# A hybrid encoder trunk on one NeuronCore: a fourth seven-product group in the feed-forward stages two to four

## The chip, the cores and the metric

The kernel runs on one core of a Trainium2 chip. The metric is the device time of one execution in microseconds, as the median of three runs. One further execution was recorded by the hardware profiler; all rows of the profile come from that one. The engines are named as the profile names them: PE (TensorE matmul), PEld (its weight load), DVE (VectorE), ACT (ScalarE), POOL (GpSimd), SP (SyncE).

## The reference

Two layers; in each a gated feed-forward block, a mixer with two kinds of attention, and a second gated feed-forward block, all on 256 tokens of width 1024 in float32, with a hidden width of 2816. Cut to what this change touches:

```python
def rms_norm(x, g):
    y = xf * lax.rsqrt(jnp.mean(xf * xf, axis=-1, keepdims=True) + RMS_EPS)
    return (y * g).astype(x.dtype)

def swiglu(h, w_gate, w_up, w_down):
    return (jax.nn.silu(h @ w_gate) * (h @ w_up)) @ w_down

for l in range(DEPTH):                                   # DEPTH = 2
    x = x + 0.5 * swiglu(rms_norm(x, ffn1_norm[l]), ffn1_w_gate[l], ffn1_w_up[l], ffn1_w_down[l])
    ...                                                  # the mixer: x = x + concat(oA, oB) @ w_out
    x = x + 0.5 * swiglu(rms_norm(x, ffn2_norm[l]), ffn2_w_gate[l], ffn2_w_up[l], ffn2_w_down[l])
return rms_norm(x, final_norm)
```

So there are four feed-forward stages: the first and second of layer 0, then the first and second of layer 1. In the profile the second lies between about 280 and 460 us, the third between about 460 and 640, the fourth from about 740 to the end.

## The kernel before

**Matmuls in three parts.** Every operand is split into a high part (rounded to fp32r) and a low part (the rest), and a product is taken as high x high + low x high + high x low. ACT makes the high part by a cast, DVE the low part by a subtraction. For a weight block the pair is one "split": `emit_split` (line 175) takes half of a raw block (two of its four 128-row slices, 128 x 1024 elements) and writes the tiles `w` from the tile `raw`. The activations are split in the same way, by `split` (line 507).

**The list of weight blocks.** All weight blocks of 512 KB to 1 MB stand in one list, `specs`, in the order in which PE uses them. `ahead` (line 212) walks through it with three pointers: it issues loads on SP (`emit_dma`, at most six raw tiles at a time), runs a block's preparation (`prep`), and splits halves, up to `look[0]` halves ahead of PE's use. It is called each time a block is taken (`weights`, line 233) and at a block's middle (`Split.part`). What it emits is placed in the queues of ACT, DVE, SP and POOL at that point of the program, and each engine keeps the program's order.

**A feed-forward stage** (`ffn`, line 567) takes the hidden width in five groups of 512 and a rest of 256. In a plain group gate and up take four blocks, each of 24 matmuls (four 128-row slices, two halves of the tokens, three parts). Then h = silu(gate) * up is made (`gate`, `hidden`), transposed on PE and split into the two tiles hT[0] and hT[1] (`turn`), and in the course of the next group two "down" blocks of 24 matmuls add hT's part of the output.

**Groups by seven products.** Groups 2, 3 and 4 compute gate and up in Strassen's way. With a = gate rows 0 to 511, d = gate rows 512 to 1023, b and c the same of up, and the tokens in two halves, seven products of 12 matmuls (`prod`, line 589) take the place of eight. `seven` (line 115) lists the blocks: a, b, d, c and a down block, then three more uses of the tile of a, which by then holds sums, and the second down block. b gets c added by a gather-add, a transfer that adds to what it finds, issued on POOL (`gather`); a gets b added in the same way; c and d are added to a by DVE (`plus`). `by_seven` (line 599) takes the products and combines them on DVE. The activations of the products with sums come from `make_sums` (line 333): four sums of quarters of x, each made on DVE, copied to its high part by ACT and reduced to its low part by DVE. They need a copy of x with its gain in float32, `copies` (line 323), eight instructions on ACT from the transposed x in PSUM. Both are done in the course of group 1, which is plain.

**Statistics of the norm.** `Norm.stats` (line 368) reduces the squares on DVE and takes the power -0.5 on POOL. This comes in the middle of group 0; the gates of group 0 use it as a scale.

**Look-ahead.** In stages two to four it is 8 halves in groups 0 to 2, 7 in group 3 and 6 in group 4; in the first stage 8 in groups 0 and 1, 6 in groups 2 and 3 and 5 in group 4.

## Time and profile before

| | |
|---|---|
| runs | 928.3, 928.95, 928.85 us; median 928.85 |
| the profiled execution | 928.39 us, span 926.6 us, granted TensorE clock 0.999 |
| DMA | 194.58 MB, mean 210 GB/s; loads on SP's queue 53.1% and gather-adds on POOL's 15.4% of the 16 engines' span |
| loads of the feed-forward weights | 1 MB each, a median of 5.3 to 5.6 us from issue to landing |
| gather-adds | 24 of 1 MB, median 10.4 us from issue to landing |

Almost every instruction has line 50, that of the helper `Kept`, through which the program calls the engines; so rows are told apart by their tiles: `ps` is PSUM, `w` a split weight half, `raw` a raw weight block, `s` a tile of activations (split x, h and hT are all of them `s`), `q` and `v` the sums of the activations, `tmp` scratch, `r` the power of the norm. A row of the timeline has start, duration, engine, line, operation, tiles (out<-in), shapes, count, and in brackets the idle time before it and what ended that. A row with a count joins equal instructions that follow each other; its duration runs from the first start to the last end. Ends of matmuls are modelled and overlap, so a rate is read from start to start.

### The profile page before, as it was taken

The numbers are of one execution on the slowest core, as the hardware profiler recorded it, in microseconds if no ns is written. First come the engines' busy times: TensorE is split into PE (matmuls) and PEld (weight loads), VectorE is DVE, ScalarE is ACT, GpSimd is POOL, SyncE is SP. The second block draws the span as 40 slices with busy tenths as digits, with TensorE's granted clock in tenths as the row PEclk, the third lists the DMA queues.
The fourth block names the chain that finished last, engine by engine and source line by source line (L and its number), as shares of the span: only waits on it lengthen the run. The fifth ranks groups of instructions, "written<-read, shape, count | busy, mean of one in ns | idle before, by whom it ended". The sixth has DMA issues, their size and how long they took to land.

```text
span 926.6 us, 12551 instructions
## 1 busy us (share of the span) xinstructions
PE 915.1 (99%) x4732; PEld 771.7 (83%) x4732; DVE 760.8 (82%) x1074; ACT 568.7 (61%) x893; POOL 59.5 (6%) x77
## 2 busy tenths in 40 slices
PE   8999999999999999999999999999999999999997
PEld 6888887899888888888888888888998888888886
DVE  6759999969876579999776799996698676799994
ACT  7836675557755557576475466565578475566561
POOL 0500000000000001000000000000001000001011
PEclk9999999999999999999999999999999999999999
DMA  9986897827434859797767597887462377597731
GB/s 338 358 224 195 253 279 262 239 98 222 135 124 167 255 152 264 188 261 270 260 234 194 144 298 204 252 279 204 114 226 92 137 231 197 143 292 221 229 118 46
DMA packets 110893, 194.58 MB, mean 210 GB/s; under 512 B 3566, under 2 KB 31280, under 8 KB 110832
## 3 DMA queue, kind: packets, MB, share of 16 engines
q1 hardware_dynamic: 96528, 166.74, 53.1%
q0 software_dynamic: 12928, 25.46, 15.4%
q10 hardware_dynamic: 1376, 1.57, 0.5%
q8 instruction: 37, 0.61, 0.3%
q14 instruction: 24, 0.20, 0.1%
HBM read 192.71 MB, written 1.05 MB: 209 GB/s over the span
## 4 chain that ended last, share of the span: by engine, by line
PE 84%; DVE 9%; issue 2%; DMA 2%; ACT 1%; POOLq 0%; ACTq 0%; POOL 0%; DVEq 0%
PE ps L50 84%; DVE w L50 6%; DMA raw<-in_ffn_w_up_dram 2%; DVE tmp L50 2%; DVE raw L50 1%; ACT w L50 1%; DVE s L50 1%; DMA xk<-in_x_dram 0%; ACT s L50 0%; DVE xk L50 0%; POOLq L1077 0%; ACTq L50 0%; ACT tmp L50 0%; POOL rf L50 0%; DVEq L50 0%
## 5 line engine op out<-in xcount | busy, mean ns | idle before, releaser
L50 PE MATMUL ps<-w,s 128*128 128x512 f32 (+1 forms) x2754 | 640.9, 391 | 0.5 <-DVE w L50 0.5
L50 PEld LDWEIGHTS ps<-w,s 128*128 128x128 f32 x2754 | 512.1, 188 | 106.5 <-DVE w L50 1.2
L50 DVE TENSOR_TENSOR w<-raw,w 128x1024 fp32r<-128x1024 f32 (+1 forms) x440 | 461.1, 1095 | 58.8 <-ACT w L50 57.8
L50 ACT CAST w<-raw 128x1024 fp32r<-128x1024 f32 (+1 forms) x440 | 390.8, 948 | 90.6 <-DVE raw L50 68.1
L50 PE MATMUL ps<-w,q 128*128 128x512 f32 x432 | 101.9, 389 | 0.0
L50 PEld LDWEIGHTS ps<-w,q 128*128 128x128 f32 x432 | 81.1, 188 | 16.8
L50 PE MATMUL ps<-s,w 128*128 128x256 f32 x672 | 84.0, 285 | 0.0
L50 PEld LDWEIGHTS ps<-s,w 128*128 128x128 f32 x672 | 81.7, 192 | 1.1
L50 ACT ACTIVATE s<-ps,gcol 128x256 fp32r<-128x256 f32 (+1 forms) x80 | 31.4, 488 | 44.6 <-PE ps L50 42.9
L50 DVE TENSOR_TENSOR raw<-raw,raw 128x1024 f32<-128x1024 f32 x48 | 56.5, 1218 | 0.0
L50 POOL DMA_DIRECT2D raw<-in_ffn_w_up_dram x24 | 31.1, 1295 | 352.5 <-DVE w L50 166.5
L50 ACT CAST s<-ps 128x512 fp32r<-128x512 f32 x44 | 23.9, 592 | 40.7 <-PE ps L50 40.7
L50 DVE TENSOR_TENSOR s<-ps,s 128x512 fp32r<-128x512 f32 x44 | 28.4, 683 | 19.9 <-ACT s L50 19.9
L50 PE MATMUL ps<-ident,s 128*128 128x128 f32 x304 | 40.5, 274 | 0.6 <-DVE s L50 0.6
L50 PEld LDWEIGHTS ps<-ident,s 128*128 128x128 f32 x304 | 35.0, 140 | 6.9 <-DVE s L50 1.5
L50 ACT ACTIVATE tmp<-tmp,r 128x512 f32<-128x512 f32 x24 | 17.3, 722 | 33.8 <-DVE tmp L50 33.8
L50 ACT ACTIVATE s<-s,negm 128x256 f32<-128x256 f32 x64 | 31.9, 501 | 6.6 <-DVE negm L50 6.4
L50 PE MATMUL ps<-w,v 128*128 128x512 f32 x144 | 34.6, 389 | 0.0
L50 ACT CAST q<-tmp 128x512 fp32r<-128x512 f32 x20 | 12.4, 621 | 35.0 <-DVE tmp L50 34.9
L50 PEld LDWEIGHTS ps<-w,v 128*128 128x128 f32 x144 | 27.0, 188 | 5.6
L50 DVE SCALAR_TENSOR_TENSOR s<-ps,gcol,s 128x256 fp32r<-128x256 f32 x48 | 20.3, 478 | 12.1 <-ACT s L50 12.0
L50 ACT COPY tmp<-ps 128x512 f32<-128x512 f32 x28 | 16.3, 583 | 22.5 <-PE ps L50 22.0
(106 smaller groups left out, 419.5 us busy)
## 6 DMA issues: line engine op xcount, KB each, us to landing
raw<-in_ffn_w_down_dram SPq DMA_DIRECT2D x44, 1024.0 KB, 5.5
raw<-in_ffn_w_gate_dram SPq DMA_DIRECT2D x39, 1024.0 KB, 5.6
raw<-in_ffn_w_up_dram SPq DMA_DIRECT2D x39, 1024.0 KB, 5.3
raw<-in_ffn_w_up_dram POOLq DMA_DIRECT2D x24, 1024.0 KB, 10.4
raw<-in_w_in_dram SPq DMA_DIRECT2D x14, 1024.0 KB, 5.4
raw<-in_ffn_w_gate_dram SPq DMA_DIRECT2D x8, 512.0 KB, 6.4
raw<-in_ffn_w_up_dram SPq DMA_DIRECT2D x8, 512.0 KB, 7.4
raw<-in_w_in_dram SPq DMA_DIRECT2D x8, 512.0 KB, 5.3
```

What stands on the lines that cost most here:

```text
L50: ins = issue(*a, **k)
```

## The change

In stages two to four group 1 is computed by seven products as well. The first stage keeps groups 2 to 4. In group 1 the order differs: a and d, the two products with plain operands, come first, then the first down block, then b + c and the others. The float32 copy of x and the first sums are made in group 0, right after the statistics; the low half of a sum comes one step after its high half. Gather-adds are held back from the start of a stage's end (or of the output projection) until the norm's power has been issued on POOL (`issue`, `flush`, `hold`). The look-ahead of groups 1 to 4 in stages two to four is 8, 7, 6 and 5 halves. There are six scratch buffers where there were five, and the squares use one of them in place of a buffer of their own.

```diff
-SEVEN = (2, 3, 4)
+SEVEN = ((2, 3, 4), (1, 2, 3, 4))
...
-        return [Step(4, 512, load(a), key=a, free=[]),
-                Step(4, 512, load(b), key=b, behind=gather(c, b), prep=gather(b, a)),
-                Step(4, 512, load(d), key=d, free=[]),
-                Step(4, 512, load(c), key=c, free=[]),
-                downs[0],
+        bc = Step(4, 512, load(b), key=b, behind=gather(c, b))
+        rest = [Step(4, 512, load(d), key=d, free=[]), Step(4, 512, load(c), key=c, free=[]), downs[0]]
+        steps = [rest[0], rest[2], bc, rest[1]] if first else [bc] + rest
+        steps[0].prep = lambda: issue(gather(b, a))
+        return [Step(4, 512, load(a), key=a, free=[])] + steps + [
                 Step(4, 512, None, src=a, free=[]),
                 Step(4, 512, None, prep=plus(c, a), src=a, free=[c]),
                 Step(4, 512, None, prep=plus(d, a), src=a, free=[a, d]),
                 downs[1]]
...
         if s.behind is not None:
-            s.behind()
+            issue(s.behind)
+    pending, hold = [], [False]
+    def issue(add):
+        pending.append(add)
+        if not hold[0]:
+            flush()
+    def flush():
+        hold[0] = False
+        while pending:
+            pending.pop(0)()
...
                 act.copy(sm[:, :, 0:P], v)
-                dve.tensor_tensor(sm[:, :, P:S], v, f(sm[:, :, 0:P]), op=ALU.subtract)
+            def low(i, v):
+                dve.tensor_tensor(self.sm[i][:, :, P:S], v, f(self.sm[i][:, :, 0:P]), op=ALU.subtract)
             s1 = make(b1, t1, ALU.subtract)
+            s2 = make(s1, t0, ALU.add)
+            low(0, s1)
             yield
-            s2 = make(s1, t0, ALU.add)
+            v = make(t1, t0, ALU.subtract)
+            low(1, s2)
             yield
...
             pool.tensor_tensor(self.r, ms, mhalf[:, 0:2], op=ALU.pow)
+            flush()
...
+            else:
+                w = weights()
+                next(sums, None)
+                p1 = prod(norm.quarter(0, 0), w)
+                hT = turn(h, (0,))
+                w = weights()
+                next(sums, None)
+                act.copy(m1, p1)
+                p2 = prod(norm.quarter(0, 1), w)
+                hT += turn(h, (1,))
+                w = weights()
+                next(sums, None)
+                g0 = put(flat(), p2, m1, ALU.add)
+                silu(g0, g0, 0)
+                down(hT, 0, 0, w)
+                act.copy(m7, prod(norm.summed(2), weights()))
+                p3 = prod(norm.summed(3), weights())
...
-        tokens(gs, norm.xs, weights(), 4)
+        w = weights()
+        sums = iter(())
+        if 1 in sevens:
+            norm.copies()
+            sums = norm.make_sums()
+        tokens(gs, norm.xs, w, 4)
         g = gate(gs)
-        tokens(us, norm.xs, weights(), 4)
+        w = weights()
+        next(sums, None)
+        tokens(us, norm.xs, w, 4)
         h = hidden(g, us)
...
-                look[0] = IN_FFN - max(0, n - 2) if before is not take_x else IN_MIX - (n == NGRP - 1)
-                h = by_seven(h, n)
+                look[0] = IN_FFN + min(sevens) - n if before is not take_x else IN_MIX - (n == NGRP - 1)
+                h = by_seven(h, n, sums)
```

More of the change, by code (lines that the diff above doesn't have):

```diff
@@ L78, in blk, with tmp @@
         return s4.tile([P, 2, 512], dt, tag="s4", name=nm_("s4"))
-    def tmp(tag="tmp", bufs=5, shape=(P, 2, 256), dt=F32):
+    def tmp(tag="tmp", bufs=6, shape=(P, 2, 256), dt=F32):
         return tp.tile(list(shape), dt, tag=tag, bufs=bufs, name=nm_(tag))
@@ L113, in plain, with seven @@
         return Step(kn, n, lambda t: [(t, src)], **how)
-    def seven(wg, wu, c0, downs):
+    def seven(wg, wu, c0, downs, first):
         a, b, c, d = [object() for _ in range(4)]
@@ L243, in trunk, with ffn_specs @@
     for l in range(DEPTH):
-        def ffn_specs(wg, wu, wd):
+        def ffn_specs(wg, wu, wd, sevens):
             down = lambda g, h: plain(wd[l], h * 512, 512, 4 * g, 4)
@@ L249, in ffn_specs @@
                 downs = [down(g - 1, h) for h in range(2)]
-                if g in SEVEN:
-                    specs.extend(seven(wg[l], wu[l], g * 512, downs))
+                if g in sevens:
+                    specs.extend(seven(wg[l], wu[l], g * 512, downs, g == 1))
                 else:
@@ L261, in ffn_specs @@
             specs.append(down(NGRP - 1, 1))
-        ffn_specs(g1, u1, d1)
+        ffn_specs(g1, u1, d1, SEVEN[l > 0])
         wi = w_in[l]
@@ L284, in trunk, with __init__ @@
         fine.update(range(mixed + 2, len(specs)))
-        ffn_specs(g2, u2, d2)
+        ffn_specs(g2, u2, d2, SEVEN[1])
     xk = const.tile([P, 2, D], F32, name="xk")
     class Norm:
-        def __init__(self, g0, sums=len(SEVEN) > 0):
+        def __init__(self, g0, sums=True):
             self.g0, self.xs, self.sums = g0, [], sums
@@ L298, in squares @@
         def squares(self, t, c, n):
-            j_ = tmp("junk", 1, (P, 512))
+            j_ = tmp().rearrange("p a n -> p (a n)")
             act.activation(j_[:, :n], xk[:, t, c:c + n], AF.Square, accum_out=self.ss[:, t, c // 256:c // 256 + 1])
@@ L344, in make @@
                 act.copy(sm[:, :, 0:P], v)
-                dve.tensor_tensor(sm[:, :, P:S], v, f(sm[:, :, 0:P]), op=ALU.subtract)
                 self.sm.append(sm)
                 return v
+            def low(i, v):
+                dve.tensor_tensor(self.sm[i][:, :, P:S], v, f(self.sm[i][:, :, 0:P]), op=ALU.subtract)
             s1 = make(b1, t1, ALU.subtract)
+            s2 = make(s1, t0, ALU.add)
+            low(0, s1)
             yield
-            s2 = make(s1, t0, ALU.add)
+            v = make(t1, t0, ALU.subtract)
+            low(1, s2)
             yield
-            make(t1, t0, ALU.subtract)
+            b0_ = make(b0, s2, ALU.subtract)
+            low(2, v)
             yield
-            make(b0, s2, ALU.subtract)
+            low(3, b0_)
             yield
@@ L565, in late, with ffn @@
                 self.nxt.stats()
-    def ffn(norm, aside=None, before=None, final=False):
+    def ffn(norm, aside=None, before=None, final=False, sevens=SEVEN[1]):
         def silu(out_, acc, t):
@@ L597, in prod, with by_seven @@
             return acc
-        def by_seven(h, g):
+        def by_seven(h, g, sums):
             flat = lambda: tmp().rearrange("p a n -> p (a n)")
@@ L608, in by_seven @@
             m1, m7 = flat(), flat()
-            act.copy(m1, prod(norm.quarter(0, 0), weights()))
-            act.copy(m7, prod(norm.summed(2), weights(held=True)))
-            hT = turn(h, 2)
-            p2 = prod(norm.quarter(0, 1), weights())
-            g0 = put(flat(), p2, m1, ALU.add)
-            p3 = prod(norm.summed(3), weights())
-            silu(g0, g0, 0)
-            down(hT, g - 1, 0, weights())
+            if g > 1:
+                act.copy(m1, prod(norm.quarter(0, 0), weights()))
+                act.copy(m7, prod(norm.summed(2), weights(held=True)))
+                hT = turn(h, 2)
+                p2 = prod(norm.quarter(0, 1), weights())
+                g0 = put(flat(), p2, m1, ALU.add)
+                p3 = prod(norm.summed(3), weights())
+                silu(g0, g0, 0)
+                down(hT, g - 1, 0, weights())
+            else:
[10 more added lines that the diff above has]
+                next(sums, None)
+                g0 = put(flat(), p2, m1, ALU.add)
+                silu(g0, g0, 0)
+                down(hT, 0, 0, w)
+                act.copy(m7, prod(norm.summed(2), weights()))
+                p3 = prod(norm.summed(3), weights())
             h = blk(F32)
             p5 = prod(norm.summed(0), weights())
-            late = g == max(SEVEN)
+            late = g == max(sevens)
             p6 = prod(norm.summed(1), weights(look[0] - 5 if late else 0, late))
@@ L636, in turn @@
             out_ = []
-            for i in range(n):
+            for i in (range(n) if isinstance(n, int) else n):
                 sl = halves(bank())
@@ L664, in ffn @@
         before(2)
-        tokens(gs, norm.xs, weights(), 4)
+        w = weights()
[4 more added lines that the diff above has]
+        tokens(gs, norm.xs, w, 4)
         g = gate(gs)
-        tokens(us, norm.xs, weights(), 4)
+        w = weights()
+        next(sums, None)
+        tokens(us, norm.xs, w, 4)
         h = hidden(g, us)
         for n in range(1, NGRP):
-            sums = norm.make_sums() if n + 1 == min(SEVEN, default=0) else iter(())
-            if n in SEVEN:
-                look[0] = IN_FFN - max(0, n - 2) if before is not take_x else IN_MIX - (n == NGRP - 1)
-                h = by_seven(h, n)
+            if n in sevens:
+                look[0] = IN_FFN + min(sevens) - n if before is not take_x else IN_MIX - (n == NGRP - 1)
+                h = by_seven(h, n, sums)
                 continue
+            sums = norm.make_sums()
             gs = [bank(), bank()]
@@ L713, in ffn_end @@
         look[0] = IN_MIX
+        hold[0] = True
         w = {0: weights()}
@@ L965, in out_part @@
             tokens(accs[h], oT, w, k0, range(2), order=order, h=h)
+        hold[0] = True
         for k0 in (0, 2, 4):
@@ L997, in trunk @@
         final = l == DEPTH - 1
-        parts = ffn(norm, attention_constants, take_x) if l == 0 else ffn(norm)
+        parts = ffn(norm, attention_constants, take_x, sevens=SEVEN[0]) if l == 0 else ffn(norm)
         norm_m = Norm(16 + l * 8, False)
```

## The prediction

> **What bounds the kernel now.** I read the page first, then the busy time by stretch, then each engine in order of time in the second feed-forward stage (280 to 460 us), the first of the three that change.

> ```profile
> span 926.6 us, 12551 instructions
> PE 915.1 (99%) x4732; PEld 771.7 (83%) x4732; DVE 760.8 (82%) x1074; ACT 568.7 (61%) x893; POOL 59.5 (6%) x77
> PE 84%; DVE 9%; issue 2%; DMA 2%; ACT 1%; POOLq 0%; ACTq 0%; POOL 0%; DVEq 0%
> ```

> PE holds 84% of the chain of waits, so a matmul taken away is time won, as long as nothing makes PE wait. DVE's 82% is a mean over unlike stretches (columns: length, then PE, PEld, DVE, ACT and POOL busy with counts):

> ```profile
> 310.00:343.50 33.50, 33.50 (x154) 27.80 (x153) 23.81 (x27) 19.34 (x29) 1.28 (x1) 1.00 0.69 186
> 374.00:405.00 31.00, 31.00 (x142) 25.76 (x141) 30.38 (x32) 19.65 (x23) 2.57 (x2) 1.00 0.80 238
> 405.00:436.00 31.00, 31.00 (x143) 25.75 (x142) 30.86 (x34) 20.11 (x24) 0.00 (x0) 1.00 0.81 246
> ```

> The first row is group 1, plain: DVE has 9.7 us to spare. The others are groups 3 and 4, already by seven products: DVE is full (30.4 and 30.9 of 31), and PE gets through them only because DVE enters with weights split ahead. The change turns the one group with a reserve into such a group.

> **What it takes away.** Group 1 in stages two to four has 84 matmuls for gate and up instead of 96.

> ```profile
> 293.42 22.03 PE L50 MATMUL ps<-w,s 128*128 128x512 f32 x96
> 315.29 1.04 PE L50 MATMUL ps<-ident,s 128*128 128x128 f32 x8
> 355.18 5.60 PE L50 MATMUL ps<-w,s 128*128 128x512 f32 x24
> 360.62 5.60 PE L50 MATMUL ps<-w,q 128*128 128x512 f32 x24
> ```

> 24 matmuls take 360.62 - 355.18 = 5.44, one 0.227; 12 are 2.72, and 36 in three stages **8.2 us**. The eight transposes stay (0.8, from 315.29 to the next matmul at 316.08).

> **What it adds.** Per stage DVE gets six more weight halves to split (18, was 12), four additions of raw weights and seven combinations of products; ACT gets six more casts and two copies; POOL two more gather-adds of 1 MB. The four sums of the activations move from the later part of group 1 to before its products. SP issues as many loads as before, with d and a down block ahead of b. DVE's rows:

> ```profile
> 301.82 2.36 DVE L50 TENSOR_TENSOR w<-raw,w 128x1024 fp32r<-128x1024 f32 x2
> 309.77 1.40 DVE L50 SCALAR_TENSOR_TENSOR s<-ps,hr,tmp 128x512 f32<-128x512 f32 x2
> 316.54 1.29 DVE L50 TENSOR_TENSOR s<-ps,s 128x512 fp32r<-128x512 f32 x2 [3.10 <-ACT s L50]
> 323.17 0.68 DVE L50 TENSOR_TENSOR tmp<-s,s 128x512 f32<-128x512 f32 x1
> 324.55 0.69 DVE L50 TENSOR_TENSOR q<-tmp,q 128x512 fp32r<-128x512 f32 x1 [0.69 <-ACT q L50]
> 352.73 2.35 DVE L50 TENSOR_TENSOR raw<-raw,raw 128x1024 f32<-128x1024 f32 x2
> 360.22 9.16 DVE L50 TENSOR_TENSOR w<-raw,w 128x1024 fp32r<-128x1024 f32 x8
> ```

> A split has its result after 1.2 and holds the queue for 1.14 (9.16 for eight); an addition of raw weights 1.15; a combination 0.6, with its result after 0.7. That is 6 x 1.14 + 4 x 1.15 + 7 x 0.6 = 15.6 us more for DVE, against the reserve of 9.7. The totals alone would cost little, since DVE also idles in group 0; what costs is the order.

> In the program as built, DVE's queue after the statistics of the norm reads: two splits of the first down block, the split of the summed block b + c, sums s1 and s2, low half of s1, second split of b + c, **then** the two products that make h of group 0, two splits of c with two more sum operations between, low half of hT[0], two splits of a + b with a sum operation and a low half, two raw additions, low half of hT[1]. PE wants h after one product, hT[0] after two, hT[1] after 12 matmuls more. Before, PE ran group 0's h through a whole plain group before hT was needed.

> And b + c is a gather-add on POOL, now held back until the norm's power has been issued there, so nothing of it moves before 301.7 (its issue takes 1.3 of POOL, which has nothing else queued but the next gathers):

> ```profile
> 301.01 0.69 POOL L50 TENSOR_TENSOR r<-ms,mhalf 128x2 f32<-128x2 f32 x1 [38.92 <-DVE ms L50]
> 307.24 1.34 POOL L50 DMA_DIRECT2D raw<-in_ffn_w_up_dram  x1 [5.53 <-DMA raw<-in_ffn_w_up_dram]
> ...
> raw<-in_ffn_w_up_dram POOLq DMA_DIRECT2D x1, 1024.0 KB, 9.3
> raw<-in_ffn_w_up_dram POOLq DMA_DIRECT2D x1, 1024.0 KB, 8.0
> raw<-in_ffn_w_up_dram POOLq DMA_DIRECT2D x1, 1024.0 KB, 14.5
> ```

> The landing rows are windows round the gathers at 307, 528 and 42 us: 9.3 with loads beside it, 8.0 the shortest, 14.5 in the first stage with a second gather 6 us behind. Here too a second one (b added to a) stands right behind. I take 9.3, nearest in place and traffic: landed at 311.0. The bounds are 309.7 and 316.2.

> [...]

> ACT's rows for the same place:

> ```profile
> 296.11 4.84 ACT L50 CAST w<-raw 128x1024 fp32r<-128x1024 f32 x5
> 303.96 1.28 ACT L50 ACT_TABLE_LOAD   x1 [3.02 <-PE ps L50]
> 305.26 1.27 ACT L50 ACTIVATE tmp<-ps,r 128x512 f32<-128x512 f32 x2
> 306.42 3.89 ACT L50 CAST w<-raw 128x1024 fp32r<-128x1024 f32 x4
> 316.88 3.04 ACT L50 ACTIVATE s<-ps,gcol 128x256 f32<-128x256 f32 x8
> 323.89 0.62 ACT L50 CAST q<-tmp 128x512 fp32r<-128x512 f32 x1 [0.92 <-DVE tmp L50]
> 346.38 0.59 ACT L50 COPY tmp<-ps 128x512 f32<-128x512 f32 x1 [3.29 <-PE ps L50]
> ```

> The eight copies of the transposed x (3.04) move to just before the gates. There ACT waits 3.02 for PE at 303.96 anyway, so I cost them at nothing; uncovered they would delay the gates by up to 3 us, which h's later wait absorbs. A cast is 1.0, a copy 0.6. From 306.5 ACT stands at the cast of b + c until it lands, and behind it stand ACT's other casts, DVE's split and, in DVE's queue, h.

> **The chain, on the clock of the second stage.** PE ends group 0 24 matmuls before 315.29, at 309.8; the first product ends at 312.5 and PE turns to h.
> - Landed 311.0; cast 1.05, split 1.2, s1 0.7, s2 0.7, copy of s2 0.6, second cast 1.05, second split 1.2, two products 1.4: h at 318.9. **Wait 1: 6.4.**
> - PE: transposes 0.4, product 2.7, transposes 0.4, at hT[0] by 322.4. DVE and ACT from 318.9: split of c 1.1, sum 0.7, its copy 0.6, cast 1.0, split 1.2, low half 0.7: 324.2. **Wait 2: 1.8.**
> - PE: 12 matmuls, 326.9. DVE and ACT from 324.2: split of a + b 1.1, sum 0.7, copy 0.6, copy of the first product 0.5, cast 1.0, split 1.2, two raw additions 2.3, low half 0.7: 332.3. PE does one matmul with the high half in between. **Wait 3: 5.2.**

> Without the ACT hand-overs in it wait 3 is still 1.1 + 0.6 + 0.6 + 1.1 + 2.3 + 0.7 = 6.4 less 2.7 = 3.7, its lower bound. After it DVE has weights ahead again: by the same addition group 2 starts with the lead that group 3 had. So groups 2 to 4 run as 3 and 4 did, with one more to eat from the lead, at 7, 6 and 5 halves of look-ahead instead of 8, 7 and 6. What a lead eaten up costs is shown by the first stage, which runs on 6, 6 and 5:

> ```profile
> 132.63 0.98 PE L50 MATMUL ps<-ident,s 128*128 128x128 f32 x7 [0.34 <-DVE s L50]
> 150.97 9.37 PE L50 MATMUL ps<-w,s 128*128 128x512 f32 x40 [0.54 <-DVE w L50]
> ```

> 0.9 us there; I take 0.5 per stage, bounds 0 and 1.5. Stages three and four have the same queues after the norm's power (rows at 479.33 and 755.95 below), so the stage counts three times. The first stage keeps groups 2 to 4; there only the sums' low halves come one step later, and a sixth scratch buffer replaces one of its own for the squares: DVE's 0.69 wait before a low half (row 324.55) may go, 0 to 0.7 per sum with PE's lead over it; I take 0.

> ```profile
> 479.33 0.71 POOL L50 TENSOR_TENSOR r<-ms,mhalf 128x2 f32<-128x2 f32 x1 [77.99 <-DVE ms L50]
> 755.95 0.70 POOL L50 TENSOR_TENSOR r<-ms,mhalf 128x2 f32<-128x2 f32 x1 [39.00 <-DVE ms L50]
> ```

> **Sum.** Per stage 6.4 + 1.8 + 5.2 + 0.5 - 2.7 = +11.2, three times +33.6. The profiled execution took 928.39 (span 926.6 and 1.8 around it), 0.46 under the median 928.85: 928.4 + 33.6 = **962 us**. Its own range: landing 1.3 earlier or 1.5 later, wait 3 at 3.7, the tail 0 to 1.5: 952 to 970.

> **Rivals.**
> - *Faster: the waits are hidden and the matmuls' time is won.* 928.4 - 8.2 = 920.2. For it: PE sets the end. It needs waits below 2.7 per stage together. Against: DVE's queue from 301.8 to hT[1] holds 8 splits, 7 sum operations, h's products, 2 low halves and 2 raw additions = 9.1 + 4.2 + 1.4 + 1.2 + 2.3 = 18.2 us without one wait, and PE is there at 309.8 + 8.9 = 318.7, so 1.3 is late already; it decides where DVE loses less than 1.4 us there to ACT and POOL. 0.05.
> - *Landed in time:* the gather is there when ACT comes, at 306.5. h at 314.4, wait 1 is 1.9: per stage 6.7, **948.5**. Against it the 8.0 row. 0.12.
> - *hT hidden, h alone waits:* 6.4 + 0.5 - 2.7 = 4.2 per stage, **941**. It needs the raw additions not to stand before hT[1]; they do in the queue. 0.08.
> - *The two gathers hold each other:* 14.5 as in the first stage, wait 1 is 11.6: 16.4 per stage, **977.6**. For it: they are 1.3 us apart (the issue row). Against: that stage also had every load of the start beside it. 0.12.

> [...] No row here shows two gathers on an idle queue.

> **How the numbers follow.** Forecast 0.60; the rest (0.03) is a lead that runs out by 3 us more per stage, 971. The range 946 to 976 holds the forecast, the gather landed in time and about half of the late one, and leaves out 0.05 + 0.08 + 0.06. Faster by over 0.2%, about what a measurement here can tell from no change: 0.05; within: 0.02; slower: 0.93.

> **What would show it.** In the changed profile: PE busy below 99% with idle time at transposes of s put down to DVE s, and at matmuls on w and s put down to DVE s, 13 us in all in each of three stages; ACT w waiting for DMA raw up for 4 to 5 us right after the gates; the gather issued right behind the power on POOL, landing 8 to 11 us later. It is wrong if PE passes h without waiting, if the first gather lands within 5 us, or if hT[1] is split before the raw additions end.

## The result, and the profile after

The changed kernel takes 962.51 us (median of five, 962.03 to 964.0); the kernel before took 928.43 beside it (five, 927.96 to 928.95). The ratio is 1.0369, 95% interval 1.0354 to 1.0384. The profiled execution took 962.03 (span 960.3, granted clock 0.981; before 926.6 and 0.999), so 33.7 us of span have to be found.

From the page the busy times and the TensorE clock in 40 slices; then the waits of PE for tiles `s`, added up (us in total, times, longest):

```profile
PE 922.1 (96%) x4696; PEld 773.5 (81%) x4696; DVE 808.6 (84%) x1125; ACT 589.6 (61%) x917; POOL 65.6 (7%) x83
PEclk9999999999999799999998999999999997999999
...
PE ps L50 <- DVE s L50: 23.9, 6, 5.2
PE ps L50 <- ACT s L50: 2.7, 3, 1.5
```

PE has 36 matmuls fewer and is nevertheless busy for 7.0 us longer than before (922.1 against 915.1). DVE is busy for 47.8 us longer (808.6 against 760.8), 15.9 per stage. Six waits for DVE and three for ACT, so three per stage, make 26.6 us of idle time. The clock row shows where the longer busy time is from: one slice in each of three places is below 9; in the kernel before, none is.

Busy time by stretch (length, then PE, PEld, DVE, ACT, POOL busy with counts, granted clock, DMA share, GB/s): groups 1 to 4 of the second stage, then group 1 of the third and fourth stage.

```profile
309.00:354.40 45.40, 37.09 (x141) 29.20 (x141) 38.76 (x43) 26.10 (x31) 2.57 (x2) 0.85 0.81 219
354.40:385.20 30.80, 30.80 (x142) 25.56 (x140) 28.33 (x29) 17.46 (x21) 2.57 (x2) 1.00 0.74 224
385.20:416.00 30.80, 30.80 (x141) 25.60 (x140) 30.70 (x32) 19.99 (x23) 2.57 (x2) 1.00 0.85 241
416.00:447.00 31.00, 31.00 (x142) 25.75 (x141) 30.56 (x33) 19.59 (x24) 0.00 (x0) 1.00 0.84 260
...
499.00:543.50 44.50, 34.97 (x141) 27.58 (x140) 37.55 (x41) 25.49 (x31) 2.57 (x2) 0.92 0.81 215
786.40:832.40 46.00, 36.90 (x141) 29.11 (x140) 38.58 (x42) 26.15 (x31) 2.57 (x2) 0.85 0.81 217
```

All of it is in group 1. From the first matmul of a group to the first of the next, group 1 took 33.57 us in each of the three stages before, and takes 45.54, 44.51 and 45.98 now: +35.3 in sum. Groups 2 to 4 stand at 30.8 as before. Back come 1.0 us in the first stage and 0.5 in the fourth group of the last.

The timeline of PE in group 1 of the second stage, and two stretches of it:

```profile
316.24 1.47 PE L50 MATMUL ps<-ident,s 128*128 128x128 f32 x4 [4.54 <-DVE s L50]
317.36 5.23 PE L50 MATMUL ps<-w,s 128*128 128x512 f32 x12
322.43 0.60 PE L50 MATMUL ps<-ident,s 128*128 128x128 f32 x4
322.78 3.02 PE L50 MATMUL ps<-w,s 128*128 128x512 f32 x12
326.31 0.51 PE L50 MATMUL ps<-w,s 128*128 128x512 f32 x1 [0.51 <-ACT s L50]
329.95 5.06 PE L50 MATMUL ps<-w,s 128*128 128x512 f32 x11 [3.14 <-DVE s L50]
334.81 3.38 PE L50 MATMUL ps<-w,q 128*128 128x512 f32 x12
338.04 2.88 PE L50 MATMUL ps<-w,v 128*128 128x512 f32 x12
...
316.00:323.00 7.00, 6.63 (x21) 5.22 (x22) 5.97 (x8) 3.00 (x4) 1.28 (x1) 0.56 0.49 160
330.00:335.00 5.00, 5.00 (x12) 3.94 (x13) 3.27 (x4) 1.66 (x2) 0.00 (x0) 0.50 0.63 210
```

PE waits 4.54 for h, then 0.51 for the high part of hT[1] and 3.14 for its low part: 8.2 together. After the waits of 4.54 and 3.14 it runs at half the clock. Twelve matmuls, 2.72 at full rate, take 322.43 - 317.36 = 5.07; eleven, 2.49 at full rate, take 334.81 - 329.95 = 4.86; the next twelve 3.23; the four transposes 1.12 where the next four take 322.78 - 322.43 = 0.35. Against full rate, and 0.4 for the transposes, that is 2.35 + 2.37 + 0.51 + 0.72 = 5.9 us more. With 2.72 saved: 8.2 + 5.9 - 2.7 = 11.4 of this stage's 11.97; 0.6 is left over. No term of the prediction had the 5.9.

ACT, POOL and the landings in the same place:

```profile
302.95 1.28 ACT L50 ACT_TABLE_LOAD   x1 [0.27 <-PE ps L50]
308.94 1.05 ACT L50 CAST w<-raw 128x1024 fp32r<-128x1024 f32 x1 [3.43 <-DMA raw<-in_ffn_w_up_dram]
...
299.85 0.70 POOL L50 TENSOR_TENSOR r<-ms,mhalf 128x2 f32<-128x2 f32 x1 [38.75 <-DVE ms L50]
300.53 2.65 POOL L50 DMA_DIRECT2D raw<-in_ffn_w_up_dram  x2
...
raw<-in_ffn_w_up_dram POOLq DMA_DIRECT2D x1, 1024.0 KB, 8.3
raw<-in_ffn_w_up_dram POOLq DMA_DIRECT2D x1, 1024.0 KB, 15.6
```

Both gather-adds go out right behind the power. The first lands 8.3 us later, at 308.9, and ACT's wait of 3.43 ends with it; the second takes 15.6. Then DVE:

```profile
310.03 1.23 DVE L50 TENSOR_TENSOR w<-raw,w 128x1024 fp32r<-128x1024 f32 x1 [6.09 <-ACT w L50]
315.35 1.40 DVE L50 SCALAR_TENSOR_TENSOR s<-ps,hr,tmp 128x512 f32<-128x512 f32 x2
321.27 0.68 DVE L50 TENSOR_TENSOR s<-ps,s 128x512 fp32r<-128x512 f32 x1
326.95 2.35 DVE L50 TENSOR_TENSOR raw<-raw,raw 128x1024 f32<-128x1024 f32 x2
329.22 0.68 DVE L50 TENSOR_TENSOR s<-ps,s 128x512 fp32r<-128x512 f32 x1
```

DVE stands idle for 6.09 us behind that cast; h (315.35) comes after both splits of b + c, and the low half of hT[1] (329.22) right after the two raw additions.

### The profile page after: what moved, and what is told of

Its sections match the earlier page's. It is cut to its first block, busy times and chain, and to the rows that moved or that the text cites. A ratio compares the mean times of both kernels' runs of the same rounds, so it can differ in the third digit from the quotient of the medians.

```text
span 960.3 us, 12597 instructions
## 1 busy us (share of the span) xinstructions
PE 922.1 (96%) x4696; PEld 773.5 (81%) x4696; DVE 808.6 (84%) x1125; ACT 589.6 (61%) x917; POOL 65.6 (7%) x83
## 3 DMA queue, kind: packets, MB, share of 16 engines
HBM read 199.00 MB, written 1.05 MB: 208 GB/s over the span
## 4 chain that ended last, share of the span: by engine, by line
PE 74%; DVE 10%; issue 7%; DMA 5%; ACT 4%; POOL 0%; POOLq 0%; ACTq 0%; DVEq 0%
PE ps L50 74%; DVE w L50 5%; DMA raw<-in_ffn_w_up_dram 4%; ACT w L50 2%; DVE tmp L50 2%; DVE raw L50 1%; DVE s L50 1%; ACT tmp L50 1%; DMA xk<-in_x_dram 0%; ACT s L50 0%; ACT q L50 0%; ACT v L50 0%; POOL rb L50 0%; DVE ss L50 0%; DVE xk L50 0%
## 5 line engine op out<-in xcount | busy, mean ns | idle before, releaser
L50 PE MATMUL ps<-w,s 128*128 128x512 f32 (+1 forms) x2574 | 614.2, 396 | 13.0 <-DVE s L50 9.4
L50 PEld LDWEIGHTS ps<-w,s 128*128 128x128 f32 x2574 | 485.1, 191 | 117.1 <-DVE s L50 10.9
L50 DVE TENSOR_TENSOR w<-raw,w 128x1024 fp32r<-128x1024 f32 (+1 forms) x458 | 484.2, 1099 | 70.5 <-ACT w L50 69.2
L50 ACT CAST w<-raw 128x1024 fp32r<-128x1024 f32 (+1 forms) x458 | 409.8, 953 | 120.7 <-DVE raw L50 85.9
L50 PE MATMUL ps<-w,q 128*128 128x512 f32 x540 | 128.2, 391 | 0.0
L50 PEld LDWEIGHTS ps<-w,q 128*128 128x128 f32 x540 | 102.3, 189 | 21.5
L50 PE MATMUL ps<-s,w 128*128 128x256 f32 x672 | 84.0, 285 | 0.0
L50 PEld LDWEIGHTS ps<-s,w 128*128 128x128 f32 x672 | 81.7, 192 | 1.1
L50 DVE TENSOR_TENSOR raw<-raw,raw 128x1024 f32<-128x1024 f32 x60 | 70.5, 1216 | 0.0
L50 POOL DMA_DIRECT2D raw<-in_ffn_w_up_dram x30 | 38.9, 1350 | 384.6 <-DVE w L50 125.0
L50 ACT ACTIVATE s<-ps,gcol 128x256 fp32r<-128x256 f32 (+1 forms) x80 | 31.4, 487 | 44.3 <-PE ps L50 42.6
L50 PE MATMUL ps<-ident,s 128*128 128x128 f32 x304 | 42.8, 280 | 14.8 <-DVE s L50 14.4
L50 PEld LDWEIGHTS ps<-ident,s 128*128 128x128 f32 x304 | 35.8, 143 | 22.4 <-issue 16.4
L50 ACT ACTIVATE tmp<-tmp,r 128x512 f32<-128x512 f32 x30 | 21.7, 722 | 49.8 <-DVE tmp L50 49.8
L50 PE MATMUL ps<-w,v 128*128 128x512 f32 x180 | 43.2, 389 | 0.0
L50 PEld LDWEIGHTS ps<-w,v 128*128 128x128 f32 x180 | 33.8, 188 | 7.0
L50 ACT COPY tmp<-ps 128x512 f32<-128x512 f32 x34 | 19.9, 584 | 26.2 <-PE ps L50 26.2
L50 ACT ACTIVATE s<-s,negm 128x256 f32<-128x256 f32 x64 | 31.9, 502 | 5.8 <-DVE negm L50 5.5
L50 DVE TENSOR_TENSOR tmp<-ps,tmp 128x512 f32<-128x512 f32 x49 | 33.4, 682 | 1.6 <-PE ps L50 1.6
L50 DVE TENSOR_TENSOR s<-ps,s 128x512 fp32r<-128x512 f32 x44 | 28.6, 681 | 7.1 <-ACT s L50 7.1
L50 ACT CAST s<-ps 128x512 fp32r<-128x512 f32 x44 | 24.2, 592 | 16.9 <-PE ps L50 16.9
L50 ACT CAST q<-tmp 128x512 fp32r<-128x512 f32 x20 | 12.4, 619 | 33.7 <-DVE tmp L50 33.2
## 6 DMA issues: line engine op xcount, KB each, us to landing
raw<-in_ffn_w_down_dram SPq DMA_DIRECT2D x44, 1024.0 KB, 6.2
raw<-in_ffn_w_gate_dram SPq DMA_DIRECT2D x39, 1024.0 KB, 5.6
raw<-in_ffn_w_up_dram SPq DMA_DIRECT2D x39, 1024.0 KB, 5.1
raw<-in_ffn_w_up_dram POOLq DMA_DIRECT2D x30, 1024.0 KB, 11.0
raw<-in_w_in_dram SPq DMA_DIRECT2D x14, 1024.0 KB, 5.2
```

The lines of the kernel that those rows point to most:

```text
L50: ins = issue(*a, **k)
```

## Experiments

The theories: *order* (PE waits because of what stands ahead of h, hT[0] and hT[1] in the queues, the late gather first of all), *amount* (DVE has more work in a stage than fits, wherever it stands), *gather alone*, and for the half clock, that it follows from idle time of PE. Times are medians beside the kernel before on the same chip (928.4 to 929.1); the 95% interval of a ratio is given where the kernel was timed more than once.

**1. The gather early.** Both places that hold it back, in `ffn_end` and at the output projection:

```diff
-        hold[0] = True
+        hold[0] = False
```

> The gather-adds of group 1 are issued when their blocks have landed instead of behind the norm's power; all else as in the changed kernel (profiled at 962.0). Theory 'order' (the waits come from what stands ahead of h and hT in the queues, the late gather being the first of these things): the gather has landed before 300, so the 3.4 us wait of ACT is gone and PE waits at most 1 us for h in each of stages two to four; the raw additions still stand ahead of hT[1], so 3 to 4 us of idle time stay there, followed by matmuls at half clock: 940 to 948. Rival 'amount' (DVE has more work than the stage holds, and what is not waited for here is waited for in groups 2 to 4): 958 or more, with new waits on w in groups 2 to 4. Rival 'gather alone' (nothing but the landing costs): 920 to 928.

948.47 us, ratio 1.0207 (1.0192 to 1.0222): 14 us less than the changed kernel, half a microsecond above the range of *order*. PE in the second stage:

```profile
312.64 0.30 PE L50 MATMUL ps<-ident,s 128*128 128x128 f32 x1 [1.00 <-DVE s L50]
313.51 3.00 PE L50 MATMUL ps<-w,s 128*128 128x512 f32 x12
318.40 2.79 PE L50 MATMUL ps<-w,s 128*128 128x512 f32 x11 [0.88 <-DVE s L50]
322.70 0.50 PE L50 MATMUL ps<-w,s 128*128 128x512 f32 x1 [1.51 <-ACT s L50]
326.35 5.06 PE L50 MATMUL ps<-w,s 128*128 128x512 f32 x11 [3.14 <-DVE s L50]
```

The wait for h is down to 1.00 and the matmuls after it run at full rate. The wait for hT[1] is untouched, the half clock behind it too (5.06). There is now a wait of 0.88 for hT[0]: in the changed kernel the slow matmuls ahead of it had covered it. *Gather alone* falls.

**2. h and hT first, the gather as late as in the changed kernel.** A shorter look-ahead at three steps lets b + c and all behind it be split after hT[1]:

```diff
-        w = weights()
+        w = weights(2, True) if 1 in sevens else weights()
         next(sums, None)
         tokens(us, norm.xs, w, 4)
...
-                w = weights()
+                w = weights(4, True)
                 next(sums, None)
                 p1 = prod(norm.quarter(0, 0), w)
                 hT = turn(h, (0,))
-                w = weights()
+                w = weights(5, True)
```

> The gather stays late; the splits of b + c and all behind them are issued after h, hT[0] and hT[1], by a shorter look-ahead at three steps. Theory 'order': no wait at the transposes of h nor at hT[0] and hT[1]; DVE comes to b + c some 7 us later and has no lead left at the fourth and seventh product, 1 to 4 us of waits on w there and in group 2: 926 to 936. Rival 'amount': the time comes back in groups 2 to 4, 952 or more. Rival 'gather alone': as the gather is as late as before, the wait moves to the product on b + c, 945 or more.

945.92, ratio 1.018 (1.0165 to 1.0195). The waits at the transposes and at hT are gone, but neither *order* nor *amount* has the number. The number lies in the range of *gather alone*, but its reason doesn't hold: the wait is not on the product with b + c.

```profile
329.51 4.30 PE L50 MATMUL ps<-w,v 128*128 128x512 f32 x11 [4.19 <-DVE v L50]
```

PE waits 4.19 for the low half of the fourth sum (v), which this edit had left behind seven splits and two raw additions, and pays for it with half a clock again (4.30 for eleven). Group 2 and the later ones are longer too, by 0.8 to 1.0 each.

**3. Both.** Early gather; b + c split in group 0, then h and hT, then the rest:

```diff
-        hold[0] = True
+        hold[0] = False
...
-                w = weights()
+                w = weights(1, True)
                 next(sums, None)
                 p1 = prod(norm.quarter(0, 0), w)
                 hT = turn(h, (0,))
-                w = weights()
+                w = weights(3, True)
```

> Early gather, b + c split in group 0 where DVE is idle, h, hT[0] and hT[1] then ahead of c, a + b and the raw additions. Theory 'order': no wait over 1 us at h, hT or in group 1, 12 matmuls fewer per stage: 920 to 925, under the kernel before. Rival 'amount': DVE has 14.7 us more work per stage than before, of which 12 us of its idle time in group 0 cannot be used since the loads bound it; the waits come in groups 2 to 4: 935 or more.

942.79, ratio 1.0155 (1.0138 to 1.0172). *Order* is wrong by 18 us, and the time lies in the range of *amount* (935 or more). The wait for v is 2.2 in each stage, and groups 2 to 4 of the second stage take 31.5, 31.5 and 31.9 where they took 30.8.

**4. Idle time of known length, in the kernel before.**

```diff
+            spare = tmp().rearrange("p a n -> p (a n)")
+            for _ in range(doses.pop(0)):           # 9, 14, 16
+                dve.tensor_tensor(spare, f(norm.xs[0][:, 0]), f(norm.xs[1][:, 0]), op=ALU.add)
         h = hidden(g, us)
```

> The kernel before with 9, 14 and 16 dummy additions (128x512) on DVE ahead of h of group 0 in stages two, three and four, so that PE stands idle at the first transpose for about 1.2, 3 and 5.4 us and nothing else changes. Theory 'the clock falls after a long enough idle time': after the longest the next 12 matmuls take about 5 us instead of 2.72 and the granted clock is about 0.5, after the shortest 2.72 and 1.0; what the middle one does is open. Total 938 from the idle time alone plus 2.4 for each stage that loses the clock: 940 to 943. Rival 'half the clock comes from something else in the changed kernel (the traffic, the new order of operands)': all three stages go on at 1.0, 938.

948.08 us in one execution, over both ranges. The dummies took 0.72 each instead of the 0.60 reckoned with, so the waits came out longer: 1.54, 3.95 and 6.63 (plus 0.2 to 0.3 at the second transpose). The three waits, then the 2.72 us in which twelve matmuls should run:

```profile
317.85 0.33 PE L50 MATMUL ps<-ident,s 128*128 128x128 f32 x1 [1.54 <-DVE s L50]
500.75 0.48 PE L50 MATMUL ps<-ident,s 128*128 128x128 f32 x1 [3.95 <-DVE s L50]
786.90 0.48 PE L50 MATMUL ps<-ident,s 128*128 128x128 f32 x1 [6.63 <-DVE s L50]
...
319.25:321.97 2.72, 2.72 (x15) 2.25 (x14) 2.67 (x4) 2.72 (x8) 0.00 (x0) 1.00 0.09 14
502.81:505.53 2.72, 2.72 (x9) 2.13 (x8) 2.01 (x3) 2.45 (x8) 0.00 (x0) 0.50 0.20 31
788.97:791.69 2.72, 2.72 (x9) 2.14 (x8) 2.00 (x3) 2.45 (x8) 0.00 (x0) 0.50 0.15 30
```

After 1.54 the clock stays at 1.00, after 3.95 and 6.63 it is 0.50, in a kernel without the change. Group 1 became 2.29, 6.86 and 9.81 longer; less the idle time that is 0.4, 2.7 and 3.0 us for the slow stretch. So here idle time alone was enough for the half clock. The other way round, experiments 5, 9 and 10 below have the matmuls and the traffic of the change but no stop of PE over 1.0 us in the three stages, and no slow stretch there. (How much idle time it takes is worked out at the end of the document.)

**5. The fourth sum earlier too.** As 3, and:

```diff
                 hT += turn(h, (1,))
-                w = weights()
                 next(sums, None)
                 g0 = put(flat(), p2, m1, ALU.add)
                 silu(g0, g0, 0)
+                w = weights()
                 down(hT, 0, 0, w)
```

> As e3_both, and the low half of the fourth sum is issued ahead of the seven splits in front of it; in e3_both the second product waited 2.2 us for it in each stage. Theory 'order': nothing stands ahead of its turn any more, so the 2.2 us go, and the half clock that followed in one stage: 933 to 937. Rival 'amount' (from 311 us on DVE is busy without a break up to the last group, 99% in groups 2 to 4 of e3_both, so PE waits for its weights a little later instead): within 2 us of e3_both's 942.8, with groups 1 to 4 of a stage together as long as in e3_both.

941.56, ratio 1.0142 (1.0127 to 1.0157): *amount*. The wait for v is gone and almost nothing is won; groups 1 to 4 of the second stage together take 131.3, in experiment 3 131.6. Group 0 and groups 1 to 4:

```profile
286.00:308.70 22.70, 22.70 (x106) 18.87 (x105) 15.95 (x23) 18.84 (x35) 2.00 (x2) 1.00 0.81 213
308.75:343.25 34.50, 31.78 (x141) 25.25 (x140) 29.92 (x33) 22.15 (x27) 2.60 (x2) 1.00 0.64 186
343.25:376.59 33.34, 31.66 (x140) 25.57 (x141) 32.89 (x35) 19.91 (x23) 2.57 (x2) 1.00 0.82 229
376.59:408.17 31.58, 31.25 (x141) 25.56 (x140) 31.47 (x33) 20.15 (x23) 2.57 (x2) 1.00 0.90 257
408.17:440.06 31.89, 31.39 (x142) 25.48 (x140) 31.45 (x34) 19.48 (x23) 0.00 (x0) 1.00 0.82 257
```

From group 2 on DVE is idle for 1.0 of 96.8 us (33.34 + 31.58 + 31.89 less its busy times), and PE waits for it in small pieces; in group 0 it is idle for 6.75 of 22.7.

**6 to 8. The raw additions on POOL,** in the changed kernel, in 5, and in the kernel before:

```diff
-                    dve.tensor_tensor(t_, t_, x_, op=ALU.add)
+                    pool.tensor_tensor(t_, t_, x_, op=ALU.add)
```

> The changed kernel with the additions of raw weights on POOL instead of DVE, in all groups by seven products; nothing else. 'Order': the additions no longer stand ahead of hT[1], so its 3.14 us wait falls to about 1 and the clock is not halved there; the wait for h stays: 947 to 954. 'Amount' adds that DVE has 4.7 us less per group and groups 2 to 4 keep their 30.8. Rival 'POOL is too slow' (an addition of 128x1024 takes over 2.4 us on it, so the chain cast, split, addition, cast of the sums of a sets the pace, or DVE's own operations get longer beside it): 960 or more.

> e5_fourth_sum with the additions of raw weights on POOL. 'Amount': DVE is the bound of e3_both and e5_fourth_sum and has 4.7 us less to do in each group by seven, so PE waits nowhere over 1 us in stages two to four: 920 to 926, under the kernel before. 'Order' alone: no more than e5_fourth_sum gained. Rival 'POOL is too slow' as in e6_pool_adds: 945 or more, with PE waiting for w whose raw block comes from POOL.

> The kernel before with the additions of raw weights on POOL. DVE is full there in groups 3 and 4 but PE waits for it only at the end of a stage (0.5 us), so no theory lets it gain more than 3 us: 926 to 929. If POOL is too slow, 935 or more.

1088.93 (one execution), 1083.81 (ratio 1.1679, 1.1659 to 1.1699) and 1027.9 (1.107, 1.1053 to 1.1086). POOL is too slow in all three, so they say nothing on *amount*. Groups of instructions (count, busy us, mean ns of one) in the kernel before with its additions on POOL:

```profile
L50 DVE TENSOR_TENSOR w<-raw,w 128x1024 fp32r<-128x1024 f32 x336 | 427.1, 1313 | 173.7 <-ACT w L50 172.4
L50 POOL TENSOR_TENSOR raw<-raw,raw 128x1024 f32<-128x1024 f32 x48 | 134.6, 2817 | 283.7 <-DVE w L50 283.7
```

and the same groups in the kernel before:

```profile
L50 DVE TENSOR_TENSOR w<-raw,w 128x1024 fp32r<-128x1024 f32 x336 | 394.0, 1219 | 53.1 <-ACT w L50 52.2
L50 DVE TENSOR_TENSOR raw<-raw,raw 128x1024 f32<-128x1024 f32 x48 | 56.5, 1218 | 0.0
```

An addition takes 2.82 us instead of 1.22, in a chain of cast, split, addition and cast that now waits for it (ACT's casts of weights for 125.7 us in sum). And of the 56.5 us taken from DVE its own splits give 33 back (427.1 against 394.0): in this trace a split or an addition begun while the other ran took longer, as the last section shows.

**9 and 10. Less work for DVE in the mended order.** In 5, `plus` does nothing, in all groups by seven (9) or in group 1 of stages two to four alone (10); the sums it makes are then left out of the computation:

```diff
             def prep():
+                return                 # 10: if first: return
```

> e5_fourth_sum without the additions of raw weights on DVE (all groups by seven; the sums a + c and a + c + d of the weights are left out of the computation), 4.7 us less on DVE per group. 'Amount': what keeps e5_fourth_sum 21 us above the 920.2 of the matmuls alone is DVE's work; with it gone 920 to 924. If something else than DVE's work holds it (the loads, ACT, the half clock): 935 or more.

> e5_fourth_sum without those additions in group 1 of stages two to four only (left out of the computation there). 'Amount': DVE has 4.7 us less per stage, and as it is busy from group 1 to the end of group 4 every one of them counts: 941.6 less 14 is 927.5, 926 to 931. If only the place of the additions in group 1 mattered, the waits in groups 2 to 4 stay and it gains under 5: 937 or more.

921.56 (ratio 0.9924, 0.991 to 0.9938) and 927.31 (0.9986, 0.9977 to 0.9995). In 10, 3 x 4.7 = 14.1 us less work on DVE make the kernel 14.2 us faster than 5: every microsecond counts. Of this, group 1 itself gives 2.0 in each stage (32.55 instead of 34.51 in the second); the rest comes in groups 2 to 4, whose own additions stayed (group 2 takes 30.84 instead of 33.34). With all additions gone only 1.4 us are left above the 920.2 of the matmuls. *Amount* holds. An addition is also a link in a chain of cast, split, addition and cast, and leaving it out shortens that chain too; in groups 2 to 4 it is DVE's work that counts, since DVE is full there and experiment 10 left their chain as it was; but for group 1, where DVE is idle for 4.6 of 34.5 us in 5, the runs don't part the two.

**11. The same work less, in the order of the change:**

> The changed kernel, its order as it is, without the additions of raw weights (left out of the computation in all groups by seven). 'Order': only the two additions that stand ahead of hT[1] count, 2.35 us of its 3.14 us wait, and the half clock behind it (2.3) may go too; the wait for h stays: 947 to 955. 'Amount' alone (the waits of the changed kernel are nothing but DVE's work): 18.8 us less on DVE per stage brings it under the kernel before, 928 or less.

955.12 (1.0284, 1.027 to 1.0298), just above the range of *order* and far from *amount* alone: PE still waits 20.7 us for s. Under the order of the change DVE has 65.6 us less to do (busy 743.0 instead of 808.6) and only 7.4 come back. The additions do stand where the prediction had them: without them the wait for the low half of hT[1] is 0.88 in each stage instead of 3.14. But the wait for h grew, to 6.30, 5.84 and 5.94 from 4.54, 4.75 and 5.16, since the first gather-add landed 9.4 to 10.2 us after its issue here, and 8.3 to 8.8 in the changed kernel. So the 7.4 are what is left after that loss. Together with 5 and 9:

| | all raw additions | none |
|---|---|---|
| order of the change | 962.5 | 955.1 |
| gather early, h, hT and the sums ahead of the splits | 941.6 | 921.6 |

**12. What else is in the change.** Group 1 plain in all stages (`SEVEN = ((2, 3, 4), (2, 3, 4))`) and nothing held back, so that the scratch buffers and the later low halves of the sums stay:

> The changed kernel with group 1 of stages two to four plain again: what is left of the change is the sixth scratch buffer, the squares in it and the low halves of the sums one step later. The first stage of the changed kernel has this and was 1.0 us shorter, the fourth group of the last stage 0.5: 926.5 to 928.5 against some 928.7 before. If that gain came from elsewhere: no difference, within 0.1%.

927.76 against 928.87 (11 and 21 executions), ratio 0.9987 (0.9978 to 0.9996): some 1 us faster, less than the 0.2% taken as the bound of what can be told, though the interval excludes 1. It is the only version with the whole computation that is not slower than the kernel before.

## Why the prediction was right, point by point

The forecast of 962 came out at 962.5. The mechanism was right as to place, sign and cause: PE waits for h and hT behind the late gather and what stands in DVE's queue. That the sum is right to a microsecond is luck. Over the three stages it had 40.2 us of idle time, 1.5 of tail and 8.2 won; measured are 26.6 of idle time, no tail, some 17 of slow matmuls and restarts (35.3 + 8.2 - 26.6), 8.2 won and 1.5 from elsewhere. Two terms were too large and one was missing, and these made up for each other.

- *Matmuls, -2.7 per stage.* Right: where nothing waits, the groups by seven take 30.8, and experiment 9 comes within 1.4 us of the sum 920.2.
- *The gather behind the power.* Right. It landed 8.3 us after its issue, not 9.3. The second one, right behind it, took 15.6 itself, while the first stayed near the 8.0 of the shortest in the kernel before and far from 14.5: the rival "hold each other" falls. "Landed in time" falls too: ACT stood at the cast for 3.43 us until the landing at 308.9.
- *Wait 1, 6.4.* Measured 4.54, 4.75 and 5.16. The landing came 1.2 us earlier, counted from the first matmul of group 1, and the chain from there to h was some 0.5 shorter. Experiment 1 shows the cause: with the gather early 1.00 is left.
- *Wait 2, 1.8.* Nothing to be seen, but not because DVE was quicker: the product ahead of hT[0] ran at half the clock, 2.35 longer. At full clock, in experiment 1, a wait of 0.88 stands there.
- *Wait 3, 5.2 (lower bound 3.7).* Measured 3.65, 4.67 and 3.82 (0.51, 1.53 and 0.68 for the high half and 3.14 for the low), at the place given: the raw additions end and hT[1] is split. Experiment 11, without the additions, has 0.88 for the low half.
- *The missing term.* The sum counted idle time alone, 13.4 per stage; it was 8.2, 9.4 and 9.0, and in the second stage 5.9 of slow matmuls came on top. The prediction's "PE: transposes 0.4, product 2.7" is the step that failed: after a wait of that length it is 1.1 and 5.1. The rows to see it were not in the trace of before.
- *The copies of x on ACT, nothing.* Right: ACT still waited 0.27 for PE behind them (row 302.95).
- *The tail, 0.5.* Measured 0. While PE waited in group 1, DVE got ahead (43 instructions in that group of the second stage, 33 in experiment 5), and groups 2 to 4 ran at 30.8.
- *The first stage, 0.* It was 1.0 shorter, inside the bound of 0 to 0.7 for each sum; experiment 12 has the same size.
- *"The totals alone would cost little ...; what costs is the order."* This is half wrong, and the right sum hides it. Mending the order takes away 20.9 of the 34; some 13 stayed in the best order tried, and experiments 9 and 10 show that they go with the additions on DVE. The step (15.6 us more against a reserve of 9.7, and idle time in group 0) counted on idle time that stayed unused: in experiment 5 DVE is full from group 2 on and still idle for 6.75 us in group 0.

The two causes do not add: the waits of the wrong order are also where DVE catches up. So leaving out the raw additions wins 7.4 us under the order of the change (after what the later gather-adds cost there) and 20 in the mended order.

What stays open: whether DVE's idle time in group 0 can be used with more raw and split buffers, which would be needed for groups 1 to 4 to run by seven without loss. It was not tried.

## What to carry to other kernels

When PE is full and a trick takes matmuls away at the price of work on another engine, look at that engine's queue twice: for what it puts ahead of the next thing PE needs, and for its total between the last point where it is idle and the end of the stretch; here mending the first (962.5 to 941.6) only uncovered the second (20.0 more without the additions). A transfer that needs nothing but its source should not be issued behind a result that comes late: here that cost 14 us (experiment 1). And a wait of PE is to be priced with the matmuls behind it: here 47 of 49 stops of 2.9 us or more, over all traces, were followed by matmuls at half the rate, shorter ones sometimes, and in the changed kernel and experiments 2 to 4 the loss was some 1.7 to 3.1 us on top of the idle time. Last, work moved from DVE to POOL is not simply gone from DVE: in experiment 8 more than half of it came back (33 of 56.5 us).

## What the hardware showed that was not expected

**The clock after a stop.** Stops of PE and the granted clock of the 2.7 to 5 us behind them: 1.00 and 1.54 us: 1.00; 2.2 us, three times in experiment 3: 0.53 once and 1.00 twice; 3.95, 4.19, 4.54 and 6.63: 0.50 to 0.56; 3.14, in all three stages of the changed kernel: eleven matmuls in 4.86, 4.12 and 4.85 instead of 2.49. The three stops of 2.2 look alike, and one of them is followed by half rate (7 matmuls in 2.75 us instead of 12).

```profile
324.98:328.39 3.41, 1.21 (x6) 0.71 (x5) 3.41 (x5) 1.05 (x1) 0.00 (x0) 1.00 0.39 66
328.39:331.80 3.41, 3.41 (x9) 2.63 (x10) 1.69 (x3) 1.66 (x2) 0.00 (x0) 0.50 0.74 276
505.88:509.30 3.42, 2.71 (x12) 1.90 (x11) 3.42 (x4) 1.05 (x1) 0.00 (x0) 1.00 0.87 159
509.30:512.71 3.41, 1.93 (x8) 1.61 (x9) 2.03 (x3) 1.35 (x2) 0.00 (x0) 1.00 0.75 232
789.18:792.60 3.42, 1.54 (x7) 0.94 (x5) 3.42 (x4) 1.05 (x1) 0.00 (x0) 1.00 0.52 89
792.60:796.01 3.41, 3.08 (x14) 2.55 (x15) 1.68 (x3) 1.66 (x2) 0.00 (x0) 1.00 0.80 289
```

The first stop lies whole in one step, which has 2.20 us of idle time, and the next step is slow; the other two are cut by a border into 0.71 and 1.48, and into 1.88 and 0.33. Counted over all fourteen traces, from 12 us on (with the modelled ends of matmuls): of the steps at full clock with 1.95 us of idle time or more, all 63 were followed by a slow one; of those with less than 1.5, none of some 2850; between 1.5 and 1.95, 15 of 41. Two stops of under 1 us did it as well: in experiment 11 stops of 0.64 and 0.88 in one step, 1.52 together, were followed by eleven matmuls in 3.98 instead of 2.49.

**POOL beside DVE.** In experiment 8 an addition of 128 x 1024 takes 2817 ns on POOL in the mean, against 1218 on DVE. The mean mixes two kinds: 27 of the 48 take 2.35 to 2.40 us, and 21, each begun while DVE was at a weight split, take 3.30 to 3.44. DVE's splits show the same from the other side: the 48 that an addition overlaps take 1.87 in the mean, the other 288 still 1.22. The 24 splits begun 1.2 us or more before the end of an addition take 2.29 to 3.05; the one at 381.75, for example, began 1.23 before that end and took 2.32. So in this trace whichever of the two began second took about as long as if it had waited for the first to end (in the example 1.23 and then 1.22, 2.45 in sum): by these times an addition moved to POOL gained next to nothing from running beside a split on DVE.

**A load beside two gather-adds.** In the second stage of the changed kernel a load of 1 MB on SP's queue, issued at 303.96 while both gather-adds were under way, took 13.2 us; the one before them, issued at 291.08, took 5.0.

```profile
raw<-in_ffn_w_down_dram SPq DMA_DIRECT2D x1, 1024.0 KB, 5.0
raw<-in_ffn_w_gate_dram SPq DMA_DIRECT2D x1, 1024.0 KB, 13.2
```
